# The rests of the weights formed by an accumulating transfer instead of a vector subtraction

## The chip, the cores and the metric

The kernel runs on one core of a Trainium2 chip. The metric is the device time of one execution in microseconds (us): the median of three runs is 1937.91 us (1937.89 to 1940.56). The engines of the core are called PE (TensorE, the matrix unit; PEld is its loading of weights), DVE (VectorE), ACT (ScalarE), POOL (GpSimd) and SP (SyncE, which here only issues transfers); transfers (DMA) are moved by 16 DMA engines of the core.

## What is computed

One inference step of a two-layer decoder trunk (width 1024) for 512 prompt tokens and 32 sample tokens (8 groups of 4), all 544 with the same weights. Every layer is a feed-forward half step, a mixer and another feed-forward half step:

```
x += 0.5 * SwiGLU_a(RMSNorm(x))    # w_in 1024 x 4096, w_out 2048 x 1024
x += Mixer_l(RMSNorm(x))           # layer 0: stick-breaking attention and RG-LRU; layer 1: gated DeltaNet
x += 0.5 * SwiGLU_b(RMSNorm(x))
SwiGLU(x): g, u = split(x @ w_in); (silu(g) * u) @ w_out
```

All is in fp32, and the results are the two sets of hidden states with the caches and states of the mixers. Nearly all arithmetic is in the products with weight matrices.

## The kernel before, in words

The tokens lie along the free dimension: the residual stream is eight tiles `x0` to `x7` of 128 features x 544 tokens. A product with a weight matrix is done in the matrix unit's fp32r type, which keeps fewer bits than fp32. So each operand is split in two: the part that fp32r holds exactly (names ending in `h`) and the rest (names ending in `l`). `mm3` (L347) multiplies three of the four combinations, per 128 input features and per half of the tokens (256, then 288): `wh*xh` (L362), `wh*xl` (L363) and `wl*xh` (L364), all into one PSUM tile `lin`.

The class `W` (L304) brings one block of weights, usually 1024 input features x 128 output features, 128 partitions x 1024 fp32, 512 KB:

- SP issues the load into a tile `raw` (L319), of which there are two buffers;
- ACT writes `wh`, the rounded copy (L323), three buffers;
- DVE writes `wl = raw - wh` (L324), two buffers.

There are 261 such blocks: 128 for the four `w_in`, 64 for the four `w_out`, 28 in the mixer of layer 0, 41 in the mixer of layer 1. The numbers of buffers are `WB = (2, 3, 2)`. A `raw` buffer may be loaded again when L324 of its block has read it; a `wl` buffer may be written again when the last L364 matmul of its block has read it.

In a feed-forward part (`ffn_body`, L383) there are first 32 blocks of `w_in`, alternately for the gate and the other branch. Each is used for both halves of the tokens and then left: 48 matmuls. Then come 8 output tiles of 16 x 128 input features, each of which needs two blocks of `w_out`; call them a and b. The order on PE is first half of the tokens: a, b; second half: a, b. So a is released three quarters of the way through its tile, b at its end.

The results leave PSUM on DVE (L401, L406, L423), the activations run on ACT (L100, L370), and the last tile's row of work (`split_x`, L267 to L273) prepares the next norm. A scheduling layer orders the instructions of each engine and places the waits; each engine then runs its own list in that order and stands still at a wait.

Of the kernel before, what the change touches and what calls it, by code (L numbers as in the profile page):

```python
# [7 lines left out]
F32 = mybir.dt.float32  # L8
# [3 lines left out]
AF = mybir.ActivationFunctionType  # L12
ALU = mybir.AluOpType
# [44 lines left out]
class Phase:  # L58
    def __init__(self, E, nf, nl):
        self.E, self.nf, self.nl = E, nf, nl  # L60
# [243 lines left out]
class W:  # L304

    def __init__(self, E, src, ks=None):
        nc = E.nc
        cols = src.shape[1]
        if ks is None:
            ks = list(range(src.shape[0] // P))  # L310
        kc = len(ks)
        v = src.rearrange("(k p) c -> p k c", p=P)
        raw = E.wp.tile([P, kc, cols], F32, tag="raw", name=E.nm("raw"), bufs=WB[0])
        a = 0
        while a < kc:
            b = a + 1
            while b < kc and ks[b] == ks[b - 1] + 1:
                b += 1
            nc.sync.dma_start(out=raw[:, a:b], in_=v[:, ks[a]:ks[b - 1] + 1])  # L319
            a = b  # L320
        self.h = E.wp.tile([P, kc, cols], F32R, tag="wh", name=E.nm("wh"), bufs=WB[1])
        self.l = E.wp.tile([P, kc, cols], F32R, tag="wl", name=E.nm("wl"), bufs=WB[2])
        nc.scalar.activation(self.h, raw, AF.Copy)  # L323
        nc.vector.tensor_tensor(self.l, raw, self.h.bitcast(F32), op=ALU.subtract)  # L324
        self.at = {k: i for i, k in enumerate(ks)}


# [1334 lines left out]
```

## Time and profile before

| what | us |
|---|---|
| median of three runs | 1937.91 |
| the profiled execution, whole | 1947.97 |
| its span in the trace | 1946.2 |
| PE busy in the span | 1897.3 |
| DVE busy | 1078.9 |
| ACT busy | 833.5 |
| POOL busy | 122.4 |

The profile is of one execution, 10 us above the median. PE is busy nearly throughout; the busy time of matmuls is that of a pipeline, in which several overlap, so the number says that PE is hardly ever without work, not that it runs at its peak. A wait is written `[idle <-releaser]`: the engine stood idle so long, and the instruction named ended it.

### The profile page before, as it was taken

What the parts mean: (1) busy time and instruction counts of PE and PEld (TensorE: products, weight loads), DVE (VectorE), ACT (ScalarE), POOL (GpSimd) and SP (SyncE); (2) the same over time, 40 slices, a digit from 0 to 9 for tenths busy, and PEclk for the clock granted to TensorE, in tenths of its full rate; (3) what the DMA queues carried; (4) which work ended last, traced back from release to release, by engine and by line L of the source; (5) the groups of instructions that cost most, each with busy time, mean ns of one, the idle gap of its engine ahead of it and who ended that gap; (6) DMA issues with size and microseconds to landing.
All of it is one profiled execution on the core that took longest, in us unless ns stands there. A gap on an engine that the chain in (4) does not pass through costs nothing.

```text
span 1946.2 us, 36314 instructions
## 1 busy us (share of the span) xinstructions
PE 1897.3 (97%) x14901; PEld 1819.1 (93%) x14901; DVE 1078.9 (55%) x2563; ACT 833.5 (43%) x1725; POOL 122.4 (6%) x234
## 2 busy tenths in 40 slices
PE   7999999999999999999999999999999999999999
PEld 6999999888768999999999999899999998999998
DVE  7444334786756444433444433788877858544422
ACT  6333324777644333323333322566574536333221
POOL 0000002111320000000000000212111100000000
PEclk8999999999999999999999999999998979999999
DMA  4333233212332333333333323333343322333332
GB/s 130 89 88 88 79 89 99 83 56 81 90 101 80 84 91 90 88 87 92 91 87 87 91 82 80 82 94 102 80 110 86 94 65 69 87 87 87 88 110 67
DMA packets 315972, 171.02 MB, mean 88 GB/s; under 512 B 28470, under 2 KB 310279, under 8 KB 315805
## 3 DMA queue, kind: packets, MB, share of 16 engines
q1 hardware_dynamic: 313244, 160.30, 29.5%
q0 software_dynamic: 2560, 8.39, 1.5%
q8 instruction: 117, 1.92, 0.4%
q14 instruction: 51, 0.41, 0.1%
HBM read 158.01 MB, written 10.65 MB: 87 GB/s over the span
## 4 chain that ended last, share of the span: by engine, by line
PE 86%; DVE 6%; ACT 4%; DMA 2%; issue 1%; POOL 1%; SPq 0%; ACTq 0%; DVEq 0%; POOLq 0%
PE lin L362 25%; PE lin L363 25%; PE lin L364 25%; PE pv L729 1%; PE s L1444 1%; DVE wl L324 1%; PE sc L758 1%; PE po L805 1%; ACT wh L323 1%; ACT f L100 0%; DMA raw<-in_w_ffn_in 0%; DVE acc L1105 0%; DVE ltmp L1222 0%; PE z L720 0%; PE m L588 0%
## 5 line engine op out<-in xcount | busy, mean ns | idle before, releaser
L362 PE MATMUL lin<-xh,wh 128*128 128x256 f32 (+2 forms) x2992 | 876.4, 293 | 16.9 <-DVE x L1555 4.2
L363 PE MATMUL lin<-xl,wh 128*128 128x256 f32 (+2 forms) x2992 | 874.7, 292 | 0.6 <-DVE xl L371 0.3
L364 PE MATMUL lin<-xh,wl 128*128 128x256 f32 (+2 forms) x2992 | 869.3, 291 | 1.5 <-DVE wl L324 1.5
L362 PEld LDWEIGHTS lin<-xh,wh 128*128 128x128 f32 (+1 forms) x2992 | 568.3, 190 | 24.1 <-ACT wh L323 8.5
L364 PEld LDWEIGHTS lin<-xh,wl 128*128 128x128 f32 (+1 forms) x2992 | 569.6, 190 | 6.7 <-issue 3.5
L363 PEld LDWEIGHTS lin<-xl,wh 128*128 128x128 f32 (+1 forms) x2992 | 568.6, 190 | 4.7 <-issue 1.7
L323 ACT ACTIVATE wh<-raw 128x1024 fp32r<-128x1024 f32 x261 | 275.6, 1057 | 507.7 <-PE lin L363 428.4
L324 DVE TENSOR_TENSOR wl<-raw,wh 128x1024 fp32r<-128x1024 f32 x261 | 317.0, 1215 | 89.9 <-PE lin L364 88.0
L362 PE MATMUL lin<-hh,wh 128*128 128x288 f32 (+1 forms) x1024 | 295.7, 289 | 0.0
L363 PE MATMUL lin<-hl,wh 128*128 128x288 f32 (+1 forms) x1024 | 295.4, 288 | 0.0
L364 PE MATMUL lin<-hh,wl 128*128 128x288 f32 (+1 forms) x1024 | 294.9, 288 | 0.0
L363 PEld LDWEIGHTS lin<-hl,wh 128*128 128x128 f32 x1024 | 193.0, 188 | 0.2
L364 PEld LDWEIGHTS lin<-hh,wl 128*128 128x128 f32 x1024 | 192.7, 188 | 0.1
L362 PEld LDWEIGHTS lin<-hh,wh 128*128 128x128 f32 x1024 | 192.5, 188 | 0.1
L401 DVE TENSOR_TENSOR sg<-lin,rstd 128x256 f32<-128x256 f32 (+1 forms) x128 | 55.8, 437 | 162.2 <-PE lin L364 162.2
L406 DVE TENSOR_TENSOR pr<-lin,rstd 128x256 f32<-128x256 f32 (+1 forms) x128 | 56.4, 441 | 155.7 <-PE lin L364 155.5
L370 ACT ACTIVATE hh<-pr 128x256 fp32r<-128x256 f32 (+1 forms) x128 | 55.1, 431 | 202.2 <-DVE pr L407 202.1
L423 DVE SCALAR_TENSOR_TENSOR x<-lin,x 128x256 f32<-128x256 f32 x64 | 28.2, 441 | 168.7 <-PE lin L364 168.7
L371 DVE TENSOR_TENSOR hl<-pr,hh 128x256 fp32r<-128x256 f32 (+1 forms) x128 | 56.5, 442 | 61.3 <-ACT hh L370 61.3
L100 ACT ACTIVATE sg<-sg 128x256 f32<-128x256 f32 (+1 forms) x128 | 53.7, 422 | 55.9 <-DVE sg L401 55.9
L267 ACT ACTIVATE xh<-x,vec 128x544 fp32r<-128x544 f32 (+2 forms) x64 | 39.6, 632 | 73.0 <-DVE x L423 59.3
L1105 DVE SCALAR_TENSOR_TENSOR acc<-XP,cw,acc 128x568 f32<-128x568 f32 x72 | 58.7, 816 | 4.0 <-ACT acc L1103 3.7
(480 smaller groups left out, 2124.8 us busy)
## 6 DMA issues: line engine op xcount, KB each, us to landing
raw<-in_w_ffn_in SPq DMA_DIRECT2D x128, 512.0 KB
raw<-in_w_ffn_out SPq DMA_DIRECT2D x64, 512.0 KB
raw<-in_w_in_odd SPq DMA_DIRECT2D x32, 512.0 KB
raw<-in_w_in_even SPq DMA_DIRECT2D x20, 512.0 KB
raw<-in_w_out_even SPq DMA_DIRECT2D x8, 512.0 KB
S<-in_state_dn_S SPq DMA_DIRECT2D x8, 512.0 KB
out_dn_S_sample<-S SPq DMA_DIRECT2D x8, 512.0 KB
raw<-in_w_out_odd SPq DMA_DIRECT2D x8, 512.0 KB
```

The costliest lines, as they stand in the source:

```text
L100: i = self.nc.scalar.activation(out, in_, func, **kw).ins
L267: nc.scalar.activation(xh, x, AF.Copy, scale=g)
L323: nc.scalar.activation(self.h, raw, AF.Copy)
L324: nc.vector.tensor_tensor(self.l, raw, self.h.bitcast(F32), op=ALU.subtract)
L362: nc.tensor.matmul(ps[:n], lhsT=wh, rhs=rh, start=(i == 0), stop=False)
L363: nc.tensor.matmul(ps[:n], lhsT=wh, rhs=rl, start=False, stop=False)
L364: nc.tensor.matmul(ps[:n], lhsT=wl, rhs=rh, start=False, stop=(i == len(terms) - 1))
L370: nc.scalar.activation(yh, src, AF.Copy)
L371: nc.vector.tensor_tensor(yl, src, yh.bitcast(F32), op=ALU.subtract)
L401: nc.vector.tensor_tensor(s, ps, E.rstd[:, c0:c0 + cn], op=ALU.mult)
L406: nc.vector.tensor_tensor(p_, ps, E.rstd[:, c0:c0 + cn], op=ALU.mult)
L1105: nc.vector.scalar_tensor_tensor(a, XP[:, j:j + XW - 3], cw[j], a, op0=ALU.mult, op1=ALU.add)
```

## The change

The rest is no longer computed by DVE. ACT copies the rounded part once more, with a factor of -1, into `wl`; then POOL issues a transfer from `raw` to `wl` that adds what it brings to what lies there, so that `wl = -wh + raw`. It holds for all 261 blocks. The numbers of buffers stay.

```
         nc.scalar.activation(self.h, raw, AF.Copy)
-        nc.vector.tensor_tensor(self.l, raw, self.h.bitcast(F32), op=ALU.subtract)
+        nc.scalar.activation(self.l, self.h.bitcast(F32), AF.Copy, scale=-1.0)
+        nc.gpsimd.dma_start(out=self.l.bitcast(F32), in_=raw, accum_op=ALU.add)
```

The new lines are L324 and L325 of the changed kernel, and the numbers of later lines rise by one. In the lists below, `[waits ...]` names the engines or transfer queues waited for: DMAHW is a transfer that SP issued, DMASW one that POOL issued. `raw`, `wh` and `wl` are as above, `hh` and `sg` activations, `x1`, `xh1` and `f` belong to the preparation of the next norm.

On ACT, in the first feed-forward part's products with `w_out`, from one output tile to the next, there stood before:

```order
L323 ACTIVATE wh_294_2699<-raw_293_2697 128x1024 [waits DMAHW6_49,PE_49,Activation_49]
L323 ACTIVATE wh_297_2705<-raw_296_2703 128x1024 [waits DMAHW7_49,PE_49,Activation_49]
L267 ACTIVATE xh1_86<-x1_78,vec_168 128x544 [waits DVE_49]
L271 ACTIVATE f_292_2692<-x1_78 128x544
L323 ACTIVATE wh_303_2816<-raw_302_2814 128x1024 [waits DMAHW0_49,PE_49,Activation_49]
```

and now stands:

```order
L323 ACTIVATE wh_294_2735<-raw_293_2733 128x1024 [waits DMAHW6_49]
L323 ACTIVATE wh_297_2742<-raw_296_2740 128x1024 [waits DMAHW7_49,PE_49,Activation_49]
L324 ACTIVATE wl_295_2736<-wh_294_2735 128x1024 [waits DMASW2_49,PE_49,Activation_49]
L324 ACTIVATE wl_298_2743<-wh_297_2742 128x1024 [waits DMASW3_49,PE_49,Activation_49]
L267 ACTIVATE xh1_86<-x1_78,vec_170 128x544 [waits DVE_49]
L271 ACTIVATE f_292_2728<-x1_78 128x544
```

The two negations of the next tile stand behind the rounding of its block b, and wait for PE to release the two `wl` buffers; the preparation of the norm stands behind them.

On DVE, at the same place, there stood before:

```order
L324 TENSOR_TENSOR wl_295_2700<-raw_293_2697,wh_294_2699 128x1024 [waits DMAHW6_49,PE_49,Activation_49]
L423 SCALAR_TENSOR_TENSOR x1_78<-lin_291_2642,x1_78 128x288 [waits PE_49]
L324 TENSOR_TENSOR wl_298_2706<-raw_296_2703,wh_297_2705 128x1024 [waits DMAHW7_49,DVE_49,Activation_49]
L268 SCALAR_TENSOR_TENSOR xl1_94<-x1_78,vec_168,xh1_86 128x544 [waits Activation_49]
L273 TENSOR_TENSOR xsq_101<-xsq_101,f_292_2692 128x544 [waits Activation_49]
```

and on POOL, whose list is empty there before, now stands:

```order
L325 DMA wl_286_2617<-raw_284_2614 128x1024 [waits DMAHW4_49,DMASW0_49,Activation_49]
L325 DMA wl_289_2624<-raw_287_2621 128x1024 [waits DMAHW5_49,DMASW1_49,Activation_49]
L325 DMA wl_295_2736<-raw_293_2733 128x1024 [waits DMAHW6_49,DMASW2_49,Activation_49]
L325 DMA wl_298_2743<-raw_296_2740 128x1024 [waits DMAHW7_49,DMASW3_49,Activation_49]
L325 DMA wl_304_2855<-raw_302_2852 128x1024 [waits DMAHW0_49,DMASW4_49,Activation_49]
```

The subtraction has left DVE, and POOL's list in the feed-forward parts holds the accumulating transfers alone, one behind the other.

On ACT, in the products with `w_in` (from the second pair of blocks to the fourth), there stood before:

```order
L323 ACTIVATE wh_113_762<-raw_112_760 128x1024 [waits DMAHW0_49,PE_49]
L370 ACTIVATE hh_51_363<-pr_95_521 128x288 [waits DVE_49]
L100 ACTIVATE sg_106_646<-sg_106_646 128x256 [waits DVE_49,Activation_49]
L323 ACTIVATE wh_116_768<-raw_115_766 128x1024 [waits DMAHW1_49,PE_49,Activation_49]
L100 ACTIVATE sg_106_646<-sg_106_646 128x288 [waits DVE_49]
```

and now stands:

```order
L323 ACTIVATE wh_113_768<-raw_112_766 128x1024 [waits DMAHW0_49]
L100 ACTIVATE sg_106_652<-sg_106_652 128x256 [waits DVE_49]
L324 ACTIVATE wl_114_769<-wh_113_768 128x1024 [waits DMASW4_49,PE_49,Activation_49]
L100 ACTIVATE sg_106_652<-sg_106_652 128x288 [waits DVE_49]
L323 ACTIVATE wh_116_775<-raw_115_773 128x1024 [waits DMAHW1_49]
```

The negation stands between the two halves of an activation, at the place in the list where PE finishes the block before the last one.

## Rows read from the trace of the kernel before

**Rows 1.** The page, part 1: busy time of each engine, its share and instructions.
```profile
PE 1897.3 (97%) x14901; PEld 1819.1 (93%) x14901; DVE 1078.9 (55%) x2563; ACT 833.5 (43%) x1725; POOL 122.4 (6%) x234
```

**Rows 2.** The page, part 4: the chain that ended last, by engine, by line.
```profile
PE 86%; DVE 6%; ACT 4%; DMA 2%; issue 1%; POOL 1%; SPq 0%; ACTq 0%; DVEq 0%; POOLq 0%
PE lin L362 25%; PE lin L363 25%; PE lin L364 25%; PE pv L729 1%; PE s L1444 1%; DVE wl L324 1%; PE sc L758 1%; PE po L805 1%; ACT wh L323 1%; ACT f L100 0%; DMA raw<-in_w_ffn_in 0%; DVE acc L1105 0%; DVE ltmp L1222 0%; PE z L720 0%; PE m L588 0%
```

**Rows 3.** The page, part 5: groups; busy us, mean ns | idle before, releaser.
```profile
L323 ACT ACTIVATE wh<-raw 128x1024 fp32r<-128x1024 f32 x261 | 275.6, 1057 | 507.7 <-PE lin L363 428.4
L324 DVE TENSOR_TENSOR wl<-raw,wh 128x1024 fp32r<-128x1024 f32 x261 | 317.0, 1215 | 89.9 <-PE lin L364 88.0
```

**Rows 4.** Windows: a w_in stretch, both mixers; stretch, busy (instructions), clock, DMA, GB/s.
```profile
40.00:200.00 160.00, 159.17 (x1269) 159.17 (x1270) 78.15 (x155) 51.95 (x85) 0.00 (x0) 1.00 0.32 89
...
300.00:640.00 340.00, 327.23 (x2229) 280.15 (x2229) 226.04 (x434) 212.15 (x415) 63.55 (x104) 0.99 0.29 83
...
1200.00:1630.00 430.00, 415.34 (x3564) 390.82 (x3563) 327.64 (x1172) 245.34 (x707) 58.57 (x125) 0.94 0.34 88
```

**Rows 5.** Timeline, w_in, ACT and PE: start us, us, instruction, [idle before <-releaser].
```profile
62.00 1.06 ACT L323 ACTIVATE wh<-raw 128x1024 fp32r<-128x1024 f32 x1 [1.71 <-PE lin L363]
...
68.03 1.06 ACT L323 ACTIVATE wh<-raw 128x1024 fp32r<-128x1024 f32 x1 [2.17 <-PE lin L363]
...
68.15 0.28 PE L364 MATMUL lin<-xh,wl 128*128 128x256 f32 x1
...
74.05 1.06 ACT L323 ACTIVATE wh<-raw 128x1024 fp32r<-128x1024 f32 x1 [1.71 <-PE lin L363]
```

**Rows 6.** Timeline, w_out, ACT, DVE, SP and PE.
```profile
228.14 1.06 ACT L323 ACTIVATE wh<-raw 128x1024 fp32r<-128x1024 f32 x1 [7.87 <-PE lin L363]
...
228.22 1.23 DVE L324 TENSOR_TENSOR wl<-raw,wh 128x1024 fp32r<-128x1024 f32 x1 [2.77 <-PE lin L364]
...
229.51 0.37 SPq L319 DMA_DIRECT2D raw<-in_w_ffn_out  x1
...
231.46 0.28 PE L364 MATMUL lin<-hh,wl 128*128 128x256 f32 x1
...
233.37 1.06 ACT L323 ACTIVATE wh<-raw 128x1024 fp32r<-128x1024 f32 x1 [0.16 <-DMA raw<-in_w_ffn_out]
...
240.34 1.23 DVE L324 TENSOR_TENSOR wl<-raw,wh 128x1024 fp32r<-128x1024 f32 x1 [2.83 <-PE lin L364]
```

**Rows 7.** The tile page: POOL's issues, ns min/median/max; their landing.
```profile
L736 POOL DMA_INDIRECT page<-in_cache_k,idx x16: 940/1041/1974, 320.9 to 531.5; - x16
L736 POOL DMA_INDIRECT page<-in_cache_v,idx x16: 942/944/951, 538.5 to 585.0; - x16
...
DMA to landing us min/median/max: 3.2/3.6/4.0
```

**Rows 8.** The page, part 3: queue, kind: packets, MB, share of 16 engines' span.
```profile
q1 hardware_dynamic: 313244, 160.30, 29.5%
q0 software_dynamic: 2560, 8.39, 1.5%
```

**Rows 9.** Windows: the first loads; columns as in rows 4.
```profile
3.00:11.00 8.00, 3.65 (x17) 3.08 (x17) 2.88 (x11) 3.80 (x12) 0.00 (x0) 1.00 1.05 343
```

**Rows 10.** Windows around an idle stretch of PE; columns as in rows 4.
```profile
1220.00:1221.00 1.00, 0.00 (x0) 0.00 (x0) 1.00 (x4) 1.00 (x2) 0.00 (x0) 1.00 0.00 0
1221.00:1222.00 1.00, 0.24 (x3) 0.22 (x3) 1.00 (x5) 0.13 (x1) 0.00 (x0) 1.00 0.00 0
...
1223.00:1224.00 1.00, 1.00 (x6) 1.00 (x7) 0.93 (x8) 0.24 (x1) 0.95 (x1) 0.65 0.00 0
1224.00:1225.00 1.00, 1.00 (x7) 1.00 (x6) 0.93 (x5) 0.24 (x1) 0.00 (x0) 0.50 0.50 72
1225.00:1226.00 1.00, 1.00 (x7) 1.00 (x7) 0.08 (x1) 0.00 (x0) 0.00 (x0) 0.50 0.91 274
1226.00:1227.00 1.00, 1.00 (x7) 1.00 (x7) 0.00 (x0) 0.00 (x0) 0.00 (x0) 0.65 0.60 179
```

## The prediction

> **What bounds the kernel now.** I read the parts of the page from the top. The first says that PE is busy for 97% of the span and no other engine for more than 55% [rows 1]. The chain of waits, followed back from the last instruction, lies on PE for 86%, almost all of it in the three matmul lines of `mm3`; the subtraction at L324 has 1% of it, about 19 us, and L323 another 1% [rows 2]. The groups tell the same from the other side: ACT's rounding and DVE's subtraction spend 276 and 317 us on 261 blocks, and what they wait for is PE [rows 3]. So DVE's work, which the change takes away, is hidden but for those 19 us, and what decides is whether PE still finds every `wl` in time. That is a matter of latency: how long it takes from PE's release of a `wl` buffer until the next block's rest lies in it.
>
> So I next read timelines of a steady stretch for each kind of product. With `w_in`, one block lasts 6.02 us on PE (ACT's waits for PE end at 62.00, 68.03 and 74.05) [rows 5]. There are two `wl` buffers, so the one released when a block ends, about 68.03, is needed by the third matmul of the block after the next: the like matmul of the block in between is at 68.15, so 68.15 + 6.02 = 74.17. With `w_out`, block a is released at three quarters of its tile: DVE, waiting for it, starts at 228.22, and the first matmul on the new `wl` of a is at 231.46, only 3.2 us later; the tiles follow each other every 12.1 us (228.22 to 240.34) [rows 6]. The subtraction of 1.23 us fits both.
>
> **What is removed, added and moved.** DVE loses 261 subtractions of 1.215 us, 317 us. ACT gets 261 copies of the form of L323, 1.057 us each [rows 3], together 276 us, and would be busy for some 1110 us of the span. Neither is a bound. The transfer is what matters. The path from release to use was one instruction; now it is: ACT's negation, POOL's issue, the transfer, its completion. Call A the time from the end of the negation until PE may use `wl`.
>
> *A from rows.* No row shows an accumulating transfer, nor one from SBUF to SBUF. The nearest are POOL's gathers of pages: 32 of them make the 8.39 MB of POOL's queue [rows 8], 256 KB each; POOL spends 0.94 to 1.04 us on an issue, and the data have landed 3.2 to 4.0 us, median 3.6, after it began [rows 7]. Ours brings 512 KB, and to add it must read 512 KB of the destination as well. The first loads, with all DMA engines full, moved 343 GB/s [rows 9]; at that rate the further 256 KB take 0.76 us and the read of the destination 1.53. A = 3.6 + 0.76 + 1.53 = 5.9 us is the value that I take, built on the median of the one row that has POOL as issuer. From below: the quickest gather, 3.2 us, with the further bytes and the read wholly overlapped. From above: SP's queue moved 160.30 MB while taking 29.5% of the engines' span [rows 8], that is 574 us or 279 GB/s. At that rate the 256 and 512 KB cost 0.94 and 1.88 us, and a load of `raw` of 512 KB in front of it another 1.88: 4.0 + 0.94 + 1.88 + 1.88 = 8.7 us.
>
> The Trainium skill has two pages on this. "Collectives: The Full Stack", The bandwidth ceiling: the fold count and why AG ≠ RS ≠ AR, says that an add in the DMA engines costs no time for the sum, but two reads for each write, so such a transfer runs at half the rate of a copy. No row here can show it. Without the second read A would be 4.4, and the sum lower by 48 us in `w_out` and 51 in `w_in`, 2096; my A counts the read. "DMA: Bandwidth & Descriptors", Anatomy of one DMA — SWDGE (gpsimd) path, gives about 2.0 us and the bytes at 436 GB/s, so an estimate of 3.2 us for 512 KB; the gathers, with half the bytes, took up to 4.0, so the trace is above it. By that page the first rival below would be the answer.
>
> *Products with `w_out`, 32 tiles.* ACT's list has the rounding of the next b ahead of the negation of a, and both wait for the same release: the rounding starts at 228.14 as now, the negation at 229.20, and ends at 230.26 [rows 6, 3]. The transfer lands at 230.26 + A = 236.2 instead of being needed at 231.46: PE stands still for A - 1.2 = 4.7 us. Block b, negated after the end of the tile (about 231.4), lands near 232.5 + A and is needed some 2.8 us into the delayed tile, so it is in time. 32 x 4.7 = 150 us.
>
> After such a stop the matrix unit is slower. PE lay idle for all of one microsecond and three quarters of the next from 1220, and its granted clock, 1.00 until then, fell to 0.65, 0.50, 0.50, 0.65 over 1223 to 1227 [rows 10], from 2.4 to 1.2 GHz: 1.7 us of work lost. Our stop is longer. 32 x 1.7 = 54 us; if the clock holds, 0.
>
> *Products with `w_in`, 128 blocks.* The negation starts with PE's release, 68.03, and ends at 69.09; the data are there at 69.09 + 5.9 = 75.0 and are needed at 74.17. That is 0.8 us for each turn of the two buffers, 64 turns: 51 us. A second circle is the `raw` buffer, which is now kept until the transfer has landed: SP's load took from 229.51 to 233.37, 3.86 us [rows 6]. Load, rounding, negation and transfer are 3.86 + 1.06 + 1.06 + 5.9 = 11.9 us, against 12.04 for two blocks: just hidden, and the next thing to be late. The idle time here is too short to count a fall of the clock.
>
> *Mixers, 69 blocks.* Their 28 and 41 blocks come every 12 and 10.5 us (340 and 430 us) [rows 4], so two take 21 to 24 us, and a circle of 13 us is hidden, except where 16 blocks of the output products follow closely: 8 x 0.8 = 6 us. DVE, busy for 226 of 340 and 328 of 430 us there [rows 4], is relieved by 69 x 1.2 = 84 us, ACT loaded with 73; I credit half of the chain's 19 us [rows 2], 10 us. POOL's list has copies and gathers that wait for DVE and PE ahead of some transfers; I have no row for the price, and put it between 0 and 1 us for each of the 69.
>
> *What stands behind the new waits.* On ACT the second half of an activation or the preparation of the next norm, due a tile later; on POOL the next transfer alone; on SP the loads, counted in the second circle. At the start the first matmul on `wl` comes later by 5.9 + 1.06 - 1.23 = 6 us. DMA engines have room: the loads take about a third [rows 4], the added transfers, at 0.76 x 2 + 1.53 = 3.1 us of each 6.02, another half.
>
> *Sum:* 150 + 54 + 51 + 6 - 10 + 6 = 257 us on the execution's 1948, which gives 2205; that execution is 10 us above the median, so 2195.
>
> **The rivals.**
>
> 1. *The transfer is quick* (A = 3.2). Only `w_out` stalls: 32 x (230.26 + 3.2 - 231.46) = 64 us, with the clock another 0 to 54; start 3, relief -10: 1995 to 2050. For it: the destination is on the chip, and reads and writes may overlap. Against it: a gather of half the size has never been quicker. 0.22.
> 2. *The adding is slow, or loads and transfers hold each other up.* At A = 8.7: 32 x 7.5 = 240 and 54 in `w_out`; 64 x 3.6 = 230 in `w_in`, and now idle stretches near those of rows 10, half of 64 x 1.7 = 54; mixers 8 x 3.6 and some waiting, 50; start 9; relief -10: 627, so 2565. For it: each load will meet a transfer under way, and nothing here shows the rate of an add. If it needed more than 6.02 - 1.88 = 4.1 us of all DMA engines per block, those would be the bound and the time beyond 2565. 0.25.
> 3. *Faster.* DVE is what the mixers wait for, and its relief of 19 us outweighs the stalls: 1919. That takes a transfer that lands within 1.2 us of the negation, since from there 230.26 + A reaches 231.46; the quickest landing is 3.2 us. 0.02.
> 4. *The time does not change*: the scheduling layer has put other matmuls into every gap. PE's list there has at most two of the second half's matmuls, 0.25 us, moved ahead, so 0.01.
>
> **How the numbers follow.** My forecast, A of 4.5 to 7.2, has 0.50: 2195 us, with its own range of 2100 to 2340. With the rivals of both lengths the range is 2030 to 2590. What this measurement can tell from no change is about 0.2%, 4 us; every case but the last two is slower by far more: faster 0.02, same 0.01, slower 0.97.
>
> **What would show it.** In the changed profile PE's idle time should be released by POOL's transfer onto `wl`, 4 to 5 us before the first L365 matmul of each `w_out` tile and under 2 us per pair in `w_in`; issues of about 1 us on POOL, landing near 5.9; L324 on ACT at 1.06; the granted clock at 0.50 after the long stops. A landing under 4.5 or over 7.2 us would make the time wrong; no waits for the transfer at all would make the whole reading wrong.

## The result and the profile after

The changed kernel takes 2296.3 us (median of four runs, 2285.5 to 2300.9) against 1939.2 before: a ratio of 1.182, 95% interval 1.177 to 1.188. The profiled execution took 2285.5 us, 337.5 more than the profiled one of before. The medians are 357 us apart: the profiled execution of before lies 9 us above its median, that of the change 11 below. The tables of stretches are of the 337.5.

The page's first part and its chain of waits stand against [rows 1, 2]:

```profile
PE 2007.0 (88%) x14901; PEld 1892.1 (83%) x14901; DVE 811.6 (36%) x2302; ACT 1070.6 (47%) x1986; POOL 319.9 (14%) x495
```

```profile
DMA 37%; PE 34%; issue 17%; ACT 7%; DVE 3%; POOL 1%; SPq 0%; POOLq 0%; ACTq 0%; DVEq 0%
DMA wl<-raw 25%; PE lin L365 10%; PE lin L363 9%; PE lin L364 9%; DMA raw<-in_w_ffn_out 7%; ACT wl L324 3%; DMA raw<-in_w_ffn_in 2%; DMA raw<-in_w_in_odd 1%; DMA raw<-in_w_in_even 1%; ACT wh L323 1%; PE pv L730 1%; PE sc L759 1%; PE s L1445 1%; POOL page L737 0%; ACT L91 0%
```

PE's share fell from 97% to 88%, and a quarter of the chain now lies on the new transfer. PE's idle time grew by 228 us (277 against 49) and its busy time by 110: its mean granted clock was 0.947 where it had been 0.982, by my estimate (span times what is missing to 1) 121 us of clock lost against 35. The groups, columns as in [rows 3]:

```profile
L365 PE MATMUL lin<-xh,wl 128*128 128x288 f32 (+2 forms) x2992 | 890.8, 298 | 116.5 <-DMA wl<-raw 115.8
...
L323 ACT ACTIVATE wh<-raw 128x1024 fp32r<-128x1024 f32 x261 | 275.5, 1056 | 844.4 <-DMA raw<-in_w_ffn_in 426.1
...
L325 POOL DMA_DIRECT2D wl<-raw x261 | 226.2, 867 | 1602.7 <-ACT wl L324 1506.6
L365 PE MATMUL lin<-hh,wl 128*128 128x256 f32 (+1 forms) x1024 | 315.9, 313 | 94.5 <-DMA wl<-raw 94.4
L324 ACT ACTIVATE wl<-wh 128x1024 fp32r<-128x1024 f32 x261 | 274.3, 1051 | 127.9 <-issue 58.5
```

PE stands still for the transfer at L365, and there alone. But the rounding at L323, which waited for PE before [rows 3], now waits for the load of `raw`: 426 us. That row is the first sign that the circle of the `raw` buffers (all that happens to a buffer from one load into it to the next), "just hidden" in the forecast, is not hidden.

The queues (q0 has POOL's transfers, q1 SP's) and the landing (the last column is the median from issue to landing, us), and windows of the first `w_in` and the first `w_out` stretch and of the two mixers, columns as in [rows 8, 4]:

```profile
q0 software_dynamic: 40144, 144.79, 33.2%
q1 hardware_dynamic: 313244, 160.30, 25.4%
...
wl<-raw POOLq DMA_DIRECT2D x260, 512.0 KB, 5.5
```

```profile
40.00:200.00 160.00, 142.88 (x1081) 138.47 (x1081) 43.89 (x120) 65.96 (x98) 19.79 (x23) 0.99 0.66 150
251.00:386.00 135.00, 110.70 (x770) 108.79 (x770) 17.32 (x32) 41.65 (x47) 13.32 (x16) 0.90 0.55 121
386.00:717.00 331.00, 302.97 (x2017) 255.36 (x2015) 183.34 (x382) 222.78 (x423) 83.77 (x133) 0.97 0.51 124
1442.00:1896.00 454.00, 411.54 (x3453) 383.01 (x3451) 293.39 (x1123) 277.90 (x740) 69.08 (x164) 0.91 0.55 126
```

From PE's timeline, by the first matmul of one kind of product to the first of the next, I took the length of each stretch in both traces. The growth in us, the four feed-forward parts in turn:

| stretch | before | growth | sum | forecast |
|---|---|---|---|---|
| `w_in` | 208.0, 193.5, 194.3, 213.2 | 32.0, 31.3, 33.1, 32.0 | 128 | 51, and 6 at the start |
| `w_out` | 96.7, 96.5, 99.5, 100.9 | 38.6, 38.7, 38.5, 36.3 | 152 | 150 + 54 |
| mixers | 312.3, 415.0 | 18.0, 39.1 | 57 | 6 - 10 |

**With `w_in`.** SP, ACT and POOL between two loads into one buffer:

```profile
71.66 0.37 SPq L319 DMA_DIRECT2D raw<-in_w_ffn_in  x1
...
76.08 1.06 ACT L323 ACTIVATE wh<-raw 128x1024 fp32r<-128x1024 f32 x1 [3.73 <-DMA raw<-in_w_ffn_in]
77.04 0.40 ACT L100 ACTIVATE sg<-sg 128x256 f32<-128x256 f32 x1
77.80 1.06 ACT L324 ACTIVATE wl<-wh 128x1024 fp32r<-128x1024 f32 x1 [0.36 <-ACT sg L100]
...
79.16 0.86 POOL L325 DMA_DIRECT2D wl<-raw  x1 [5.99 <-ACT wl L324]
...
85.00 0.37 SPq L319 DMA_DIRECT2D raw<-in_w_ffn_in  x1
```

Load until 76.08, rounding, half an activation, negation until 78.86, transfer until SP, 0.05 us after the landing, issues the next load at 85.00. Nothing in this circle waits for PE. Over 24 blocks it took 13.9 us on average, against 12.05 in which PE uses two blocks: a load of 4.6, gap between rounding and negation of 0.7, and 6.5 from the end of the negation to the landing.

**With `w_out`.** One tile (the L365 row is the first that needs the new `wl` of a), and windows of 1 us around it:

```profile
281.34 1.06 ACT L323 ACTIVATE wh<-raw 128x1024 fp32r<-128x1024 f32 x1 [4.00 <-PE lin L364]
282.31 1.04 ACT L324 ACTIVATE wl<-wh 128x1024 fp32r<-128x1024 f32 x1
283.64 0.86 POOL L325 DMA_DIRECT2D wl<-raw  x1 [13.71 <-ACT wl L324]
...
288.22 0.39 PE L365 MATMUL lin<-hh,wl 128*128 128x256 f32 x1 [3.13 <-DMA wl<-raw]
```

```profile
284.00:285.00 1.00, 1.00 (x9) 0.86 (x7) 0.37 (x1) 0.32 (x1) 0.51 (x1) 1.00 0.00 0
...
286.00:287.00 1.00, 0.00 (x0) 0.00 (x0) 0.59 (x1) 0.92 (x2) 0.86 (x1) 1.00 1.04 197
287.00:288.00 1.00, 0.00 (x0) 0.00 (x0) 0.83 (x2) 0.00 (x0) 0.00 (x0) 1.00 1.08 197
288.00:289.00 1.00, 0.78 (x6) 0.78 (x7) 0.00 (x0) 0.00 (x0) 0.00 (x0) 0.94 1.01 197
289.00:290.00 1.00, 1.00 (x6) 1.00 (x6) 0.00 (x0) 0.00 (x0) 0.00 (x0) 0.50 1.29 197
290.00:291.00 1.00, 1.00 (x6) 1.00 (x6) 0.00 (x0) 0.00 (x0) 0.00 (x0) 0.50 0.65 71
291.00:292.00 1.00, 1.00 (x7) 1.00 (x6) 0.00 (x0) 0.00 (x0) 0.00 (x0) 0.50 1.08 317
```

This is the stop that the forecast described, rounding of b ahead of the negation of a and all. It is 3.1 us, and then PE's clock is at 0.50 for three microseconds, 6 or 7 matmuls in each where a microsecond before the stop has 9. Over the whole of this `w_out` stretch the clock is 0.90 (the window 251 to 386 above). Tiles follow every 17.0 us instead of 12.1.

### The profile page after: what moved, and what is told of

Same layout as the page of the kernel before. It is cut to its first block, busy times and chain, and to the rows that moved or that the text cites. A ratio compares the mean times of both kernels' runs of the same rounds, so it can differ in the third digit from the quotient of the medians.

```text
span 2283.7 us, 36771 instructions
## 1 busy us (share of the span) xinstructions
PE 2007.0 (88%) x14901; PEld 1892.1 (83%) x14901; DVE 811.6 (36%) x2302; ACT 1070.6 (47%) x1986; POOL 319.9 (14%) x495
## 4 chain that ended last, share of the span: by engine, by line
DMA 37%; PE 34%; issue 17%; ACT 7%; DVE 3%; POOL 1%; SPq 0%; POOLq 0%; ACTq 0%; DVEq 0%
DMA wl<-raw 25%; PE lin L365 10%; PE lin L363 9%; PE lin L364 9%; DMA raw<-in_w_ffn_out 7%; ACT wl L324 3%; DMA raw<-in_w_ffn_in 2%; DMA raw<-in_w_in_odd 1%; DMA raw<-in_w_in_even 1%; ACT wh L323 1%; PE pv L730 1%; PE sc L759 1%; PE s L1445 1%; POOL page L737 0%; ACT L91 0%
## 5 line engine op out<-in xcount | busy, mean ns | idle before, releaser
L365 PE MATMUL lin<-xh,wl 128*128 128x288 f32 (+2 forms) x2992 | 890.8, 298 | 116.5 <-DMA wl<-raw 115.8
L363 PE MATMUL lin<-xh,wh 128*128 128x288 f32 (+2 forms) x2992 | 882.3, 295 | 13.5 <-ACT wh L323 3.7
L364 PE MATMUL lin<-xl,wh 128*128 128x288 f32 (+2 forms) x2992 | 880.8, 294 | 0.0
L365 PEld LDWEIGHTS lin<-xh,wl 128*128 128x128 f32 (+1 forms) x2992 | 573.9, 192 | 148.3 <-DMA wl<-raw 144.9
L323 ACT ACTIVATE wh<-raw 128x1024 fp32r<-128x1024 f32 x261 | 275.5, 1056 | 844.4 <-DMA raw<-in_w_ffn_in 426.1
L325 POOL DMA_DIRECT2D wl<-raw x261 | 226.2, 867 | 1602.7 <-ACT wl L324 1506.6
L365 PE MATMUL lin<-hh,wl 128*128 128x256 f32 (+1 forms) x1024 | 315.9, 313 | 94.5 <-DMA wl<-raw 94.4
L324 ACT ACTIVATE wl<-wh 128x1024 fp32r<-128x1024 f32 x261 | 274.3, 1051 | 127.9 <-issue 58.5
L363 PE MATMUL lin<-hh,wh 128*128 128x256 f32 (+1 forms) x1024 | 315.7, 310 | 0.0
L364 PE MATMUL lin<-hl,wh 128*128 128x256 f32 (+1 forms) x1024 | 314.2, 308 | 0.0
L365 PEld LDWEIGHTS lin<-hh,wl 128*128 128x128 f32 x1024 | 213.0, 210 | 103.0 <-DMA wl<-raw 102.9
L363 PEld LDWEIGHTS lin<-hh,wh 128*128 128x128 f32 x1024 | 215.1, 210 | 0.2
L408 DVE TENSOR_TENSOR pr<-pr,sg 128x256 f32<-128x256 f32 (+1 forms) x128 | 56.5, 442 | 9.4 <-ACT sg L100 0.5
```

Source lines behind the costliest of these rows:

```text
L324: nc.scalar.activation(self.l, self.h.bitcast(F32), AF.Copy, scale=-1.0)
L325: nc.gpsimd.dma_start(out=self.l.bitcast(F32), in_=raw, accum_op=ALU.add)
L363: nc.tensor.matmul(ps[:n], lhsT=wh, rhs=rh, start=(i == 0), stop=False)
L364: nc.tensor.matmul(ps[:n], lhsT=wh, rhs=rl, start=False, stop=False)
L365: nc.tensor.matmul(ps[:n], lhsT=wl, rhs=rh, start=False, stop=(i == len(terms) - 1))
L408: nc.vector.tensor_tensor(p_, p_, sg[:, c0:c0 + cn], op=ALU.mult)
```

## The experiments

Growth in us against the stretches of before, each from one profile; the ratio is that of all runs, with its interval. Parts that are the same in two kernels differ by up to 9 us here (the mixer of layer 0 in `e7` and `e8`, the first `w_in` in `e7` and `e9`, the four `w_out` in `e4` and `e5`), so less than that says nothing.

| kernel | median us | ratio | `w_in` | `w_out` | mixer 0, 1 |
|---|---|---|---|---|---|
| the change | 2296.3 | 1.182 (1.177 to 1.188) | 128 | 152 | 18, 39 |
| `e1_raw3` | 2322.2 | 1.196 (1.194 to 1.198) | 146 | 165 | 18, 49 |
| `e2_wl3` | 2182.8 | 1.126 (1.123 to 1.129) | 90 | 71 | 23, 37 |
| `e3_dveadd` | 1971.4 | 1.016 (1.014 to 1.019) | 5 | 4 | 12, 3 |
| `e4_copy` | 2047.6 | 1.056 (1.052 to 1.059) | 6 | 58 | 4, 33 |
| `e5_actq` | 2069.1 | 1.065 (1.063 to 1.067) | 12 | 67 | 17, 34 |
| `e6_both` | 2068.4 | 1.066 (1.062 to 1.070) | 21 | 45 | 14, 40 |
| `e7_negraw` | 2273.0 | 1.172 (1.169 to 1.175) | 124 | 159 | 7, 30 |
| `e8_oddraw3` | 2293.7 | 1.180 (1.173 to 1.187) | 133 | 152 | 15, 47 |
| `e9_oddwl3` | 2259.3 | 1.164 (1.162 to 1.166) | 124 | 157 | 15, 9 |
| `e10_all` | 2044.1 | 1.052 (1.048 to 1.056) | 22 | 45 | 11, 19 |
| `e11_allcopy` | 1971.9 | 1.017 (1.015 to 1.019) | 9 | 11 | -2, -4 |

**Is it the transfer at all?** `e3_dveadd`:

```
-        nc.gpsimd.dma_start(out=self.l.bitcast(F32), in_=raw, accum_op=ALU.add)
+        nc.vector.tensor_tensor(self.l, self.l.bitcast(F32), raw, op=ALU.add)
```

> ACT negates as in the changed kernel, but DVE adds raw onto the negation in place of the transfer. Theory A (the latency of the transfer is the whole loss, ACT's 261 extra copies are hidden): rounding, negation and addition of 1.06, 1.06 and 1.2 us take 3.3 us from the release with w_out, where 3.2 were to be had: 0 to 10 us above the kernel before, 1938 to 1950 us. Rival D (the extra copies in ACT's list, and its busy time of 1070 us, cost much by themselves): a third or more of the loss stays, over 2050 us.

1971 us. Nine tenths of the loss go with the transfer. It is 21 to 33 us more than I expected: by the profile 15 of 24 us lie in the mixers. Whether ACT's extra copies cost this, or the path from rounding to rest, which is longer by a negation here too, no run separates.

**What does the add cost?** `e4_copy` drops `accum_op=ALU.add` from that line.

> The transfer copies raw onto wl without adding; the subtraction is thus left out of the computation, everything else stays (negation, issue, order, buffers). It shows what the add costs. Theory E (an add reads its destination too, so that its engines need twice a copy's time): 4 KB packets take half of the 0.34 us, the transfer lands 1.4 us earlier, 3.4 instead of 4.8 us after the negation where it runs alone; 64 pairs x 1.4 with w_in = 90, 32 tiles x 1.4 to 2.5 with w_out (the stop of 3.1 us becomes 1.7, and part of the clock's fall goes) = 45 to 80, mixers 15: 2100 to 2150 us. Rival F (issue and completion are what takes long, the add is free): packets and landing as before, 2275 to 2300 us.

2048 us, below the range of theory E: 249 us of the change's 357 hang on the add. The queues of this kernel, to be read against those above, and its issue on POOL:

```profile
q1 hardware_dynamic: 313244, 160.30, 28.0%
q0 software_dynamic: 40032, 144.79, 19.2%
...
wl<-raw POOLq DMA_DIRECT2D x260, 512.0 KB, 3.2
```

```profile
L325 POOL DMA_DIRECT2D wl<-raw x261 | 139.1, 533 | 1456.2 <-ACT wl L324 1403.1 <-DMA raw<-in_w_ffn_in 15.0 <-ACT junk L1158 10.3
```

And a window of 1 us in its first `w_out` stretch, in which a copy has the DMA engines for itself:

```profile
275.00:276.00 1.00, 0.21 (x2) 0.00 (x0) 0.21 (x1) 1.00 (x2) 0.00 (x0) 1.00 1.02 414
```

Without the gathers (1.5% of 1946 us [rows 8], 29 us) the change's transfers took 0.332 x 2283.7 - 29 = 729 us of all engines, the copies 0.192 x 2046.6 - 29 = 364: 2.8 and 1.4 us for 512 KB, a factor of 2.0. The windows say the same: with the engines full the copy moves 414 GB/s, the adding transfer 197 (286 to 289 us above). Landing is 2.3 us earlier, more than these 1.4; the shorter issue, 0.53 instead of 0.87 us, gives another 0.3. That the rest comes of fewer transfers meeting others is my reading and not shown.

The Trainium skill, "Collectives: The Full Stack", The bandwidth ceiling: the fold count and why AG ≠ RS ≠ AR, says of a ReduceScatter that it runs at about half the rate of an AllGather, which only copies, because its add needs two source reads. The factor of 2.0 agrees with it. By the Trainium skill, "DMA: Bandwidth & Descriptors", Anatomy of one DMA — SWDGE (gpsimd) path, 2.0 us and the bytes at 436 GB/s make an estimate of 3.2 us for 512 KB. The copy's median agrees with it; the adding transfer is 2.3 us above it.

**Which circle?** `e1_raw3` and `e2_wl3` give a third buffer, from the feed-forward part's own memory, to `raw` or to `wl`:

```
+def third(E, tag, shape, dt, name, n):
+    fp = getattr(E, "third", {}).get(tag)
+    if fp is not None:
+        E.turn = getattr(E, "turn", 0) + 1
+        if E.turn % 3 == 0:
+            return fp.tile(shape, dt, tag=tag + "x", name=E.nm(name), bufs=1)
+    return E.wp.tile(shape, dt, tag=tag, name=E.nm(name), bufs=n)
-        raw = E.wp.tile([P, kc, cols], F32, tag="raw", name=E.nm("raw"), bufs=WB[0])
+        raw = third(E, "raw", [P, kc, cols], F32, "raw", WB[0])
```

> The changed kernel with a third raw buffer in the four feed-forward parts alone, wh and wl as they are. Theory A (what is late with w_in is the circle of the two raw buffers: each load is issued 0.05 us after the landing of the transfer before the last one, and load 4.4, rounding 1.06, negation 1.06 with waits of 0.7 and 0.3, landing 6.2 make 14 us for two blocks instead of 12.05): loads come early, ACT's wait of the rounding for the load goes, and only the circle of the two wl buffers is left, 0.8 to 1.4 us per pair instead of 2.0. 64 pairs x 0.6 to 1.2 = 40 to 75 us less: 2215 to 2255 us, with w_out tiles still 17.0 us apart. Theory B (loads and transfers fill the DMA engines and hold each other up): the pair with w_in stays at 14 us, 2280 to 2300. Theory C (the two wl buffers are what is late): no change either, 2280 to 2300.

> The changed kernel with a third wl buffer in the four feed-forward parts alone, raw and wh as they are. Theory A (raw circle with w_in, wl circle with w_out): w_in parts unchanged at 225 to 227 us; a w_out tile is bound by its raw circle instead of its wl buffer, 14 to 14.5 us instead of 17.0, and the stops are too short to take the clock down: 32 x 2.5 to 3 = 80 to 95 us less, 2190 to 2215 us. Theory B (DMA engines full): nothing changes, or w_out falls by a little: 2260 to 2300. Theory C (wl buffers alone are late everywhere): both products lose their waits, 129 and 152 us less: about 2010 us.

`e2_wl3` came out 7 us under theory A's range, and its `w_out` part as that theory has it: 71 instead of 152. But `w_in`, which the theory left as it was, fell from 128 to 90, so the `wl` buffers are late there too. Its raw circle in `w_in`, from load to load of one buffer, is 82.47 to 96.08, 13.6 us:

```profile
82.47 0.37 SPq L328 DMA_DIRECT2D raw<-in_w_ffn_in  x1
...
89.05 1.06 ACT L332 ACTIVATE wh<-raw 128x1024 fp32r<-128x1024 f32 x1 [7.31 <-DMA raw<-in_w_ffn_in]
90.14 1.06 ACT L333 ACTIVATE wl<-wh 128x1024 fp32r<-128x1024 f32 x1
...
91.49 0.86 POOL L334 DMA_DIRECT2D wl<-raw  x1 [8.91 <-ACT wl L333]
...
96.08 0.37 SPq L328 DMA_DIRECT2D raw<-in_w_ffn_in  x1
```

`e1_raw3` missed: it did not gain but lost. Its ACT shows why:

```profile
84.52 1.06 ACT L332 ACTIVATE wh<-raw 128x1024 fp32r<-128x1024 f32 x1 [1.70 <-PE lin L373]
85.49 1.04 ACT L333 ACTIVATE wl<-wh 128x1024 fp32r<-128x1024 f32 x1
```

The rounding waits for PE again and no longer for the load, so the raw circle is open. But with `raw` early, the scheduling layer put the rounding of a later block, which needs a `wh` that PE releases, ahead of the negation, as it does with `w_out`. So the `wl` circle has one rounding more: release 84.5, negation ended 86.53, landing 5.6 us later, 7.6 us in all where 6.1 were to be had. Both circles are thus late with `w_in`; opening one uncovers the other, and here with a rounding added. That is my theory A corrected, and theory B is not yet excluded by it.

`e6_both` opens both, by a like `third` and with two `wh` there, and makes the negation from `raw`:

```
+        nc.scalar.activation(self.l, raw, AF.Copy, scale=-1.0)
+        nc.gpsimd.dma_start(out=self.l.bitcast(F32), in_=raw, accum_op=ALU.add)
         nc.scalar.activation(self.h, raw, AF.Copy)
-        nc.scalar.activation(self.l, self.h.bitcast(F32), AF.Copy, scale=-1.0)
-        nc.gpsimd.dma_start(out=self.l.bitcast(F32), in_=raw, accum_op=ALU.add)
```

> The accumulating transfer with three raw and three wl buffers in the feed-forward parts (two wh there, to make room; in the mixers the numbers stay), and with the negation made from raw itself, ahead of the rounding, so that it doesn't wait for wh. Theory A (two circles of latency: the raw buffers with w_in, the wl buffers with w_out; either alone keeps the loss, as the runs with one more buffer of one kind showed): with both opened, 18 us are there for a circle of 14, so the products lose nearly all: w_in 0 to 20 us over before in all, w_out 0 to 20, mixers 55 to 65 as they were: 2000 to 2045 us. Theory B (loads and adding transfers hold each other up in the DMA engines, which were busy for 0.73 with three wl buffers): more buffers only queue more transfers; at least half of the 90 and 71 us that were left with three wl buffers stay: over 2080 us.

2068 us, between the ranges of the two theories, but the feed-forward parts fell from 280 to 66 us of growth. A window of `w_in`:

```profile
60.00:180.00 120.00, 120.00 (x958) 120.00 (x958) 35.33 (x80) 55.20 (x80) 17.22 (x20) 1.00 0.82 175
```

PE is busy for 120 of 120 us while loads and adding transfers take 0.82 of the DMA engines. So theory B, the engines as the bound, falls for `w_in`; the loss there is latency in circles of too few buffers.

`e7_negraw` is only the edit just shown, with the buffers as in the change:

> The changed kernel, its numbers of buffers kept, with the negation made from raw itself (rounded as wh is) and ahead of the rounding of wh in the code. Theory A: the circle of the raw buffers is shorter by one rounding, 1.06 us, and by the wait behind it, 0.3 to 0.7: 64 pairs x 1.1 to 1.7 = 70 to 110 us less with w_in; with w_out the negation of the next a no longer stands behind the rounding of b, 1.06 us and a part of the clock's fall: 32 x 1.06 to 1.8 = 34 to 58 us less. 2120 to 2190 us; if the negation keeps its place behind an activation on ACT, half of it. Theory B (DMA engines): 2275 to 2300 us, as the changed kernel.

2273 us, 1% below the change and outside theory A's range. The scheduling layer kept the rounding ahead of the negation in these stretches (rounding 80.35, negation 81.90 with `w_in`; rounding of b 275.47, negation of a 276.44 with `w_out`), so the circle was not shortened, and the run doesn't test what it was to test. It shows that this edit brings 1% without the buffers. What it does along with them is not shown: in `e6_both` the negation does run ahead, with `w_in` starting some 5 us before its block's rounding, and no run has three of both buffers without the edit.

**The mixers.** `e5_actq`, with the copy of `e4_copy`, takes the waiting transfers out of POOL's list there (`in_ffn` is set in the feed-forward parts):

```
-        nc.gpsimd.dma_start(out=self.l.bitcast(F32), in_=raw, accum_op=ALU.add)
+        (nc.gpsimd if getattr(E, "in_ffn", False) else nc.scalar).dma_start(out=self.l.bitcast(F32), in_=raw)
```

> As e4_copy (raw copied onto wl, the subtraction left out of the computation), but in the two mixers ACT's queue issues the copies, right behind its negation, and POOL's list holds its own work alone there; in the feed-forward parts POOL issues as before. In e4_copy the mixer of layer 1 was 33 us longer than before the change, and that of layer 0 4 us. Theory P (a transfer that waits on POOL for its negation holds up POOL's small copies behind it, and these hold DVE and PE): the mixer of layer 1 loses 20 to 30 of its 33 us, the whole time is 2015 to 2030. Rival R (what costs there is that the raw buffer is kept until the copy has landed, 3.2 us longer than by a subtraction): nothing changes, 2040 to 2055. Rival S (ACT, whose list is full there, pays for the issues): slower than e4_copy, over 2055.

2069 us, above `e4_copy`, as rival S had it; the mixer of layer 1 keeps its 34 us and that of layer 0 is 13 us longer. Theory P falls for the mixer of layer 1, unless ACT's issues cost there just what POOL's list had cost. In the mixer of layer 0 the trace of the change does show POOL's list:

```profile
550.98 1.21 POOL L737 DMA_INDIRECT page<-in_cache_k,idx  x1 [3.76 <-PE tp L752]
551.35 1.04 ACT L324 ACTIVATE wl<-wh 128x1024 fp32r<-128x1024 f32 x1
...
552.72 1.87 POOL L737 DMA_INDIRECT page<-in_cache_k,idx  x1 [0.16 <-issue]
554.90 1.45 POOL L737 DMA_INDIRECT page<-in_cache_k,idx  x1 [0.30 <-issue]
...
557.64 0.98 POOL L325 DMA_DIRECT2D wl<-raw  x1
...
562.31 0.58 PE L365 MATMUL lin<-xh,wl 128*128 128x256 f32 x1 [11.61 <-DMA wl<-raw]
```

The negation ends at 552.39, but three issues of gathers and small copies stand ahead of the transfer in POOL's list: it is issued 5.2 us late, and PE stands still for 11.6 us, the longest of all its waits for a transfer. In `e4_copy` this stop is 9.8 us, in `e5_actq` it is gone; but that mixer grew by only 4 us in the one and by 17 in the other, so what the list costs in all is not shown. `e8_oddraw3` and `e9_oddwl3` give a third buffer there, by `third` with the condition

```
+    if tag == ("raw" if E.odd else "wh"):
```

in the first and "wl" in place of "raw" in the second (`E.odd` is set in that mixer).

> As e7_negraw, with a third raw buffer in the mixer of layer 1 alone (and two wh there instead of three, to make room). In e7_negraw that mixer was 30 us longer than before the change. Theory R (the raw buffer, kept until the transfer has landed, makes the next load and with it the next wl late there): the mixer loses 15 to 30 of the 30 us, 2243 to 2260 us in all. Rival W (the wl buffers are late there): the mixer stays 25 to 40 us longer, 2265 to 2285 us. Rival L (what costs there is that one block is asked for only when the one before it is near its end, so that latency shows whatever the buffers): no change here nor with a third wl.

> As e7_negraw, with a third wl buffer in the mixer of layer 1 alone (and two wh there). Theory R: the mixer keeps its 30 us, 2265 to 2285 us. Rival W: it loses 15 to 30 us, 2243 to 2260 us. Rival L: no change.

Both start from `e7_negraw`, whose mixer of layer 1 is 30 us over before. With a third `raw` that mixer is no shorter (47 us over before), with a third `wl` it is 9 us over, and the whole 1.4% shorter than with the third `raw`, well outside both intervals. It is rival W. What PE waited for the transfer in that mixer, in the change and in `e9_oddwl3` (us, times, longest):

```profile
PE lin L365 <- DMA wl<-raw: 15.0, 13, 3.3
```

```profile
PE lin L374 <- DMA wl<-raw: 2.8, 2, 2.2
```

In `e7_negraw` these waits are 8.9 us, so they give back only 6 of the 21 us. More comes from the granted clock, in the mixer of layer 1 of `e7_negraw` and of `e9_oddwl3`:

```profile
1432.00:1877.00 445.00, 406.85 (x3454) 382.06 (x3455) 292.33 (x1125) 277.86 (x741) 68.24 (x164) 0.93 0.56 129
```

```profile
1441.00:1865.00 424.00, 397.98 (x3453) 372.43 (x3452) 289.43 (x1120) 275.46 (x737) 68.97 (x165) 0.95 0.60 138
```

At 0.93 of 445 us some 31 us are lost, at 0.95 of 424 some 21, so by this estimate 10 of the 21 us are the clock's.

**All of it together.** `e10_all` is `e6_both` with the third `wl` of `e9_oddwl3`; `e11_allcopy` is that without the add.

> e6_both (three raw and three wl buffers in the feed-forward parts, negation from raw) and in the mixer of layer 1 the third wl buffer of e9_oddwl3. If the two are independent, the mixer of layer 1 falls from 40 us above before to 9 to 20, and the rest stays as in e6_both: 2068 - 20 to 31 = 2037 to 2050 us. Rival: the mixer's gain was one of the order that the scheduling layer happened to choose, and doesn't come back: 2060 to 2080 us.

> e10_all with a copy in place of the adding transfer (the subtraction is left out of the computation). It tells what is left of the loss beside the time of the add. Theory A (what is left in the feed-forward parts, 66 us, is still the transfer's length, 5.6 us against 3.2): feed-forward parts 0 to 15 us above before, mixers 10 to 30: 1955 to 1985 us. Rival D (what is left comes of ACT's list with its 261 negations and of the transfers' places in it): feed-forward parts keep 40 us or more: 2010 us and above.

2044 and 1972 us, both in the ranges expected, the second not by its parts (feed-forward 20 where 0 to 15 were expected, mixers -6 where 10 to 30 were). The gains add up, and what is left in the feed-forward parts, 67 us, is for two thirds the add's time, since with a copy 20 are left. None of these kernels beats the one before; even the copy, with these circles open, is 1.7% slower.

## Why the prediction was right and where not

The direction, the mechanism and the range were right: 2296 us lies in 2030 to 2590. The time is 101 us above the 2195 forecast: 257 us were forecast to be added, 337.5 came in the profile. Three terms were off, not all to one side: `w_in` and the mixers came out 77 and 61 us above their terms, `w_out` 52 below. That the sum missed by only 80 us is in part luck.

- *A.* 5.9 us from the end of the negation to use; measured 0.3 to the issue and 5.5 to the landing at the median, 5.8. The value held, its make-up only in the sum: without the second read 4.4 was forecast, and the copy took 0.3 + 3.2 = 3.5; the read was set at 1.5, and the add cost 2.3. That these cancel is luck. And it is not one value: 4.8 for a in `w_out`, whose transfer begins with the DMA engines idle, 5.7 to 6.0 for b behind it, 6.5 in `w_in` beside the loads.
- *`w_out`, forecast 150 + 54, measured 152.* The stop is A - 1.7 with A = 4.8, 3.1 us instead of 4.7. The clock's fall was sized right: 17.0 - 12.1 - 3.1 = 1.8 us for each tile, where 1.7 were set. It is gone in the first `w_out` stretch of `e2_wl3`, whose longest stop is 1.7 us (window below); in the second and third, where stops of up to 3.2 us were left, the clock was 0.96 and 0.93.

```profile
260.00:340.00 80.00, 72.19 (x552) 69.80 (x551) 12.14 (x22) 29.48 (x34) 9.46 (x11) 1.00 0.72 154
```

- *`w_in`, forecast 51, measured 128.* The step that failed is the second circle: "Load, rounding, negation and transfer are 3.86 + 1.06 + 1.06 + 5.9 = 11.9 us, against 12.04 for two blocks: just hidden". Measured: 4.6 + 1.06 + 0.7 + 1.06 + 6.5 + 0.05, some 14 us. The transfer was set 0.6 us too short, the 0.7 us between rounding and negation at nothing, and the load 0.7 too short. By the traces the transfers did not lengthen these loads: 3.86 is the shortest that ended a wait with `w_out`, and with `w_in` in the trace of before the shortest of all is 4.0 us:

```profile
1650.62 0.37 SPq L319 DMA_DIRECT2D raw<-in_w_ffn_in  x1
...
1654.62 1.06 ACT L323 ACTIVATE wh<-raw 128x1024 fp32r<-128x1024 f32 x1 [0.39 <-DMA raw<-in_w_ffn_in]
```

Where the rounding waited for the load, the mean is 4.6 us in both traces (15 times before, 115 after). With 4.0 the forecast's own sum is 12.0, so its margin of 0.1 us was none. The clock, for which nothing was set with `w_in`, took by the estimate some 10 of the 128 us (0.983 on average over the four stretches, against 0.994 before).
- *Mixers, forecast -4, measured 57.* I took a circle of 13 us to be hidden where two blocks come in 21 to 24. On average they do; but in the mixer of layer 1 PE waits for the transfer, and there the third `wl` brought 21 of 30 us back (`e7`, `e9`), about half of it through the clock. For the fall of the clock in the mixers nothing was set; at 0.97 and 0.91, where [rows 4] have 0.99 and 0.94, it took some 20 of the 57 us. POOL's list, which I could not price, held one transfer up for 5.2 us of the longest stop, 11.6 us, in the mixer of layer 0. The credit for DVE's relief stays unproven: with a copy and these circles open the mixers are 6 us shorter than before, which is within the 9 us.
- *Start, forecast 6.* Not seen as a term of its own: the first `w_in` grew like the others.
- *The rivals.* The quick transfer fell: it would have needed a landing of 3.2, which only the copy has; with the copy `w_out` grew by 58 us, where that rival had 64. Of the second rival half is true: the transfers are longer beside loads, and with `w_out` the loads beside transfers (5.3 us where a rounding waited, against 4.2), but as a bound they don't appear, as `e6_both` shows. Of the signs named, PE's wait before L365 in a `w_out` tile was 3.1 us and not 4 to 5; issue, L324 and clock were as named.

Left open: the mixer of layer 1 loses 33 us to a copy that lands in 3.2 us and hardly more, 39, to the transfer that lands in 5.5. By the same estimate 19 of the 33 and 15 of the 39 are the clock's (0.90 of 448 us with the copy, 0.91 of 454 with the transfer, 0.94 of 430 before); why it fell more with the quicker transfer stays open. So does what the rest of the mixer of layer 0's 18 us is due to.

## What to carry to other kernels

When one engine's instruction becomes a transfer, count every buffer that the transfer now holds, write down the circle of each (load, compute, issue, landing, next load), and take the durations from the stretch in question, with the waits between the steps and the new traffic beside them; a circle that fits by 0.1 us in such a sum is not hidden. Look at the list of the engine that issues the transfer, too: what stands ahead of it there is part of the path. Before adding a buffer look for the next circle behind it and for the order the scheduler will then choose: one more `raw` alone made this kernel slower; one more of both, with the negation made from `raw`, took away three quarters of the loss in these parts. Here an adding transfer was a slow way to save an instruction on an engine that wasn't the bound.

## What the runs showed of the hardware

- An adding transfer within the chip's memory held the DMA engines 2.0 times as long as a copy of the same 512 KB (2.8 against 1.4 us; 197 against 414 GB/s with the engines full), and its issue cost POOL 0.87 against 0.53 us.
- The landing of such a transfer was 4.5 us from its issue with idle engines and 5.5 at the median. Loads took no longer beside transfers with `w_in` (4.6 us to the rounding that waited, in both traces), but did with `w_out` (5.3 against 4.2) and in `e2_wl3` (6.6 us from 82.47 to 89.05 in the lines above).
- The granted clock fell to 0.50 for three microseconds after a stop of 3.1 us in `w_out`, and was 0.90 or 0.91 over each of the four `w_out` stretches; in the first of `e2_wl3`, whose longest stop was 1.7 us, it stayed at 1.00.
